# Moving the first block's modulation into the mixing, an embedding's projection ahead of the FFN, and all splits to VectorE

## The chip, the cores and the metric

The kernel runs on one core of a Trainium2 chip. The metric is the device time of one execution in microseconds, the median of several runs. TensorE (PE in the profile) multiplies, with a separate row for its weight loads (PEld); VectorE (DVE), ScalarE (ACT) and GpSimd (POOL) work on elements; SyncE (SP) issues most transfers, GpSimd some.

## What is computed

Two blocks, each with two layers, on 256 tokens of 1024 features. The first block has a mixing layer (a bidirectional scan beside a long convolution) and a neighbourhood attention, each followed by a convolutional FFN and a per-layer embedding. The second block has a context of its own, and everything in it is modulated by a vector computed from a condition:

```python
def conv_ffn(h, norm_g, w_up, conv_w, conv_b, w_down):
    u = dwconv_centred(rmsnorm(h, norm_g) @ w_up, conv_w, conv_b)
    return (jax.nn.gelu(u[..., :D_FF]) * u[..., D_FF:]) @ w_down

def per_layer_embedding(h, p_i, norm_g, w_gate, w_proj):
    return jax.nn.sigmoid(rmsnorm(h, norm_g) @ w_gate) * (p_i @ w_proj)

def half_ffn(h, g, shift, scale, gate, wg, wu, wd):
    return h + 0.5 * gate * swiglu(modulate(rms_norm(h, g), shift, scale), wg, wu, wd)
...
    for l in range(DEPTH):
        ml = jnp.split(s_lat @ w_mod[l] + b_mod[l], N_MOD, axis=-1)
        mc = jnp.split(s_ctx @ w_mod[l] + b_mod[l], N_MOD, axis=-1)
        x = half_ffn(x, g_norm[l, 0], ml[0], ml[1], ml[2], ...)
        ctx = half_ffn(ctx, g_norm[l, 0], mc[0], mc[1], mc[2], ...)
```

The context's first half FFN needs nothing of the first block, so its work can be laid beside that block's. The modulation has 2 x 9 x 1024 results for two conditions; a unit of it is 256 results of a layer, so there are 36 units in a layer.

## The kernel before

Activations lie with features on partitions, as eight tiles of 128 features by 256 tokens. A weight arrives as float32 in a tile `raw`, and is split (`split`, L358) into a rounded high part `wh`, a cast on ScalarE (L359), and a rest `wl` (L360), a subtraction on VectorE or GpSimd. Each step over 128 inputs is three products, high by high, high by low and low by high (`gemm`, L368 to L370; for four tiles at once `gemm_wide`, L406 to L408). Some weights are used unsplit, in plain float32 (`plain_tiles`, L372, and `plain`, L397). An output tile over eight such steps is 24 products, a pair of them 48.

The stages in order are the mixing (0 to 546 us of the trace), the first FFN (to 770), its embedding (to 834), the attention (to 1018), the second FFN (to 1235), its embedding (to 1286), and from there the second block. Behind the mixing's scan, from about 334 us, the context's half FFN runs as filler (`ctx_ffn`, L948, tiles named `fill`). It is a generator that yields after each group of `FILL`: pairs of up tiles, then eight down tiles. In the mixing the loop at L935 takes `CUT` = 4 groups; the rest is drained behind ple1 (L1484 and after), and lies beside the stages between as their scheduler places it. The order of each engine's queue comes from a scheduler at build time; on the chip each queue runs in that order, and instructions wait for their operands and for a free buffer.

In the mixing the split weights of the filler use two buffers each, `wh` and `wl`, in the pool `self.wha` (`whl_open(es, 2, 0)`, L1456); after the mixing the filler has its own pool (`self.own`), and there GpSimd does its subtraction (L360). GpSimd also does half of the subtractions of the first four weight tiles of a stage (`first`, `relief`, L348 to L353), and the sums of squares for the next norm (`sq_add`, L496).

The modulation (`mod_until`, L1004) loads a tile of w_mod, 128x1024, and reduces it against a condition on VectorE (L1032). Two variants are in use. In the mixing `mod_open(pool, aid=False, room=self.wha)` (L847) takes buffers of the same pool as the filler's weights, issues loads on GpSimd's queue (L1029) and makes two reductions for a tile, one for each condition. In the FFNs `aid` is on: the loads are SyncE's, VectorE makes one reduction, and GpSimd multiplies (L1036) and ScalarE sums (L1037) for the second condition. Twelve units are done in the mixing, eight in the first FFN (to 20), six in the second (to 26).

The embedding (`embed`, L572) splits its 256 inputs `p` and the projection's weights, makes the projection `pj` at the start of its stage (16 steps, 48 products), and then the gate's products behind its norm. A norm is a sum over partitions (L454), a chain of small operations for the root (L424 to L441), a transposition (L480), and the scaling (L519).

Of the kernel before, what the change touches and what calls it, by code (L numbers as in the profile page):

```python
# [17 lines left out]
P = 128  # L18
D = 1024
T = 256  # L20
KT = 8
FF = 2816
FT = 22
# [6 lines left out]
M00 = 32  # L30
CUT = 4
DECAY = math.exp(-0.5)

# [239 lines left out]
class Net:  # L273
# [35 lines left out]
    def pieces(self, name, todo):  # L309

        nc, arr = self.nc, self.ap[name]
        i = 0
        while i < len(todo):
# [34 lines left out]
    def first(self, it, n):  # L348

        self.relief = 2  # L350
        tiles = [next(it)[1:] for _ in range(n)]
        self.relief = 0
        return tiles  # L353

    def wtiles(self, name, tiles, kt):
        return self.pieces(name, [(t, 0, kt) for t in tiles])

    def split(self, src, hi, lo, pool=False):  # L358
# [13 lines left out]
    def plain_tiles(self, name, todo):  # L372
# [4 lines left out]
        while i < len(todo):  # L377
# [6 lines left out]
            for c in range(0, n, 512):  # L384
                w = min(512, n - c)
                raw = self.t(self.whole, [P, 512], "raw")
# [100 lines left out]
    def sq_add(self, m, s=0):  # L487
# [43 lines left out]

    def conv_ffn(self, i, mods):
        nc = self.nc
        with ExitStack() as es:
            pool = self.pool(es, "ffn")
            self.whl_open(es, 0, 3)
            it = self.wtiles(f"f_up{i}", range(2 * FT), KT)
            first = self.first(it, 4)
            xh, xl = self.norm1(pool, f"ffn_norm{i}")
            self.mod_open(pool, True)  # L540
            mod0 = self.mod_at
            outs = [self.acc()[:, :T] for _ in range(4)]
            self.gemm_wide(outs, first, KT, xh, xl)
            for k0, kn in GROUPS:
                mh = self.t(pool, [P, 8, T], "mh", F32R)
                ml = self.t(pool, [P, 8, T], "ml", F32R)
                for j in range(kn):
# [14 lines left out]
                    self.split(u[:, 0], mh[:, j], ml[:, j])  # L562
                    if k0 + j > 1:
                        self.mod_until(mod0 + (mods - mod0) * (k0 + j) // (FT - 1))
                for m, wh, wl in self.pieces(f"f_dn{i}", [(m, k0, kn) for m in range(KT)]):
# [3 lines left out]
                    if k0 == 16:  # L569
                        self.sq_add(m)  # L570

    def embed(self, i):  # L572
        nc = self.nc
        with ExitStack() as es:
            pool = self.pool(es, "ple")
            self.whl_open(es, 0, 3)
            ph = self.t(pool, [P, 2, T], "ph", F32R)
            pl = self.t(pool, [P, 2, T], "pl", F32R)
            pr = self.t(pool, [P, 2, T], "pr")
            nc.sync.dma_start(pr, self.ap[f"p{i}"])  # L580
            self.split(pr, ph, pl)
            pj = self.t(pool, [P, KT, T], "pj")
            m = 0
            for _, wh, wl in self.pieces(f"ple_p{i}", [(t, 0, 2) for t in range(KT)]):
                ps = self.acc()
                self.gemm(ps[:, :T], wh, wl, 2, ph, pl)
                nc.scalar.mul(pj[:, m], ps[:, :T], 0.5)
                m += 1
            it = self.wtiles(f"ple_g{i}", range(KT), KT)
# [4 lines left out]
            for m in range(KT):  # L594
# [7 lines left out]
                nc.scalar.activation(s, ps, AF.Tanh, scale=0.5)  # L602
                nc.vector.scalar_tensor_tensor(s, s, 1.0, pj[:, m], op0=ALU.add, op1=ALU.mult)
                nc.vector.tensor_add(self.H[:, m], self.H[:, m], s)
# [234 lines left out]
    def mix(self, ef):  # L839
# [4 lines left out]
        with ExitStack() as es:  # L844
# [4 lines left out]
            with ExitStack() as e2:  # L849
# [587 lines left out]
    def run(self, es, stages=None):  # L1437
# [13 lines left out]
        self.own, self.tables = None, False  # L1451
        self.nsplit = self.relief = 0
        self.spare = []
# [15 lines left out]
        self.nrm = self.pool(es, "nrm", bufs=6)  # L1469
        self.rsp = self.pool(es, "rsp", bufs=2)  # L1470
        ep = es.enter_context(ExitStack())
        self.psum_open(ep, mm=4, aux=2, fill=2)
# [9 lines left out]
        for s in st:  # L1482
            if s.startswith("ffn"):
                self.conv_ffn(int(s[3]), 20 if s == "ffn0" else 26)  # L1484
            elif s.startswith("ple"):
                self.embed(int(s[3]))
                if s == "ple1" and self.own:
                    self.tag = self.aux = "fill"
# [4 lines left out]
                    ep.close()  # L1493
                    self.psum_open(es, mm=5, aux=3)
            elif s == "na":
                self.na()
# [262 lines left out]
```

## Time and profile before

| | us |
|---|---|
| median of three runs | 2905.65 (2905.5 to 2906.85) |
| the profiled execution | 2907.19 |
| its span in the profile | 2905.4 |
| TensorE busy in it | 2767.0 |
| VectorE busy | 1978.3 |
| ScalarE busy | 1216.2 |
| GpSimd busy | 396.7 |
| mean share of the clock that TensorE was granted | 0.97 |

The page gives busy time by engine, slices of the span with the granted clock, the chain that ended last, the costliest groups of instructions and the transfers. The trace behind it answers narrower questions: busy time in given stretches, who ended whose waits, the instructions of a line, and the instructions in order of time. The granted clock is a share of 2.4 GHz; 0.5 is the lower level of 1.2 GHz.

### The profile page before, as it was taken

The numbers are of one execution on the slowest core, as the hardware profiler recorded it, in microseconds if no ns is written. First come the engines' busy times: TensorE is split into PE (matmuls) and PEld (weight loads), VectorE is DVE, ScalarE is ACT, GpSimd is POOL, SyncE is SP. The second block draws the span as 40 slices with busy tenths as digits, with TensorE's granted clock in tenths as the row PEclk, the third lists the DMA queues.
The fourth block names the chain that finished last, engine by engine and source line by source line (L and its number), as shares of the span: only waits on it lengthen the run. The fifth ranks groups of instructions, "written<-read, shape, count | busy, mean of one in ns | idle before, by whom it ended". The sixth has DMA issues, their size and how long they took to land.

```text
span 2905.4 us, 49052 instructions
## 1 busy us (share of the span) xinstructions
PE 2767.0 (95%) x19514; PEld 2441.6 (84%) x19514; DVE 1978.3 (68%) x3569; ACT 1216.2 (42%) x2120; POOL 396.7 (14%) x276
## 2 busy tenths in 40 slices
PE   6998999899999989989999999999999999999999
PEld 4676788899899889979988669888898888895999
DVE  5875755789976688867754665777755655567655
ACT  3212223555545555555554454222243222455543
POOL 0100000322542411221211001000010000121100
PEclk8998999999999999989999999999999999999999
DMA  4441223666455356547732103555535444230564
GB/s 164 126 141 58 81 83 117 211 214 221 165 179 159 107 189 203 185 142 241 223 113 68 47 30 119 186 196 179 163 110 164 141 142 134 79 117 25 175 188 139
DMA packets 150807, 415.91 MB, mean 143 GB/s; under 512 B 31585, under 2 KB 51698, under 8 KB 149682
## 3 DMA queue, kind: packets, MB, share of 16 engines
q1 hardware_dynamic: 146258, 393.89, 42.3%
q0 software_dynamic: 4320, 18.88, 1.9%
q8 instruction: 154, 2.52, 0.4%
q14 instruction: 75, 0.61, 0.1%
HBM read 411.66 MB, written 1.05 MB: 142 GB/s over the span
## 4 chain that ended last, share of the span: by engine, by line
PE 73%; DVE 8%; issue 4%; ACT 2%; DMA 1%; POOL 0%; ACTq 0%; DVEq 0%; SPq 0%; POOLq 0%
PE mm L368 18%; PE mm L370 18%; PE mm L369 18%; DVE wl L360 3%; PE fill L370 2%; PE fill L368 2%; PE mm L407 2%; PE mm L1413 2%; PE fill L369 2%; PE mm L408 2%; PE mm L406 2%; PE mm L1381 1%; PE aux L459 1%; ACT wh L359 1%; PE aux L1407 1%
## 5 line engine op out<-in xcount | busy, mean ns | idle before, releaser
L359 ACT CAST wh<-raw 128x1024 fp32r<-128x1024 f32 (+3 forms) x652 | 606.8, 938 | 1016.3 <-PE mm L369 560.8
L360 DVE TENSOR_TENSOR wl<-raw,wh 128x1024 fp32r<-128x1024 f32 (+3 forms) x582 | 712.6, 1228 | 321.3 <-ACT wh L359 308.4
L368 PE MATMUL mm<-xnh,wh 128*128 128x256 f32 (+1 forms) x2592 | 821.4, 317 | 4.2 <-ACT u L527 3.2
L370 PE MATMUL mm<-xnh,wl 128*128 128x256 f32 (+1 forms) x2592 | 818.5, 316 | 1.9 <-DVE wl L360 1.9
L369 PE MATMUL mm<-xnl,wh 128*128 128x256 f32 (+1 forms) x2592 | 815.5, 315 | 0.4 <-DVE xnl L360 0.2
L368 PEld LDWEIGHTS mm<-xnh,wh 128*128 128x128 f32 x2592 | 488.3, 188 | 38.3 <-ACT u L527 3.4
L370 PEld LDWEIGHTS mm<-xnh,wl 128*128 128x128 f32 x2592 | 488.3, 188 | 37.9 <-DVE wl L360 2.9
L369 PEld LDWEIGHTS mm<-xnl,wh 128*128 128x128 f32 x2592 | 487.9, 188 | 34.4 <-DVE xnl L360 1.0
L369 PE MATMUL mm<-ml,wh 128*128 128x256 f32 (+1 forms) x1104 | 341.3, 311 | 10.8 <-DVE ml L360 10.8
L368 PE MATMUL mm<-mh,wh 128*128 128x256 f32 (+1 forms) x1104 | 340.5, 314 | 5.0 <-ACT mh L359 2.1
L370 PE MATMUL mm<-mh,wl 128*128 128x256 f32 (+1 forms) x1104 | 341.0, 312 | 0.0
L1032 DVE CUSTOM_DVE_ANT_0 junk<-wm,sc,vecs 128x1024 bf16<-128x1024 f32 x200 | 256.8, 1284 | 4.2 <-ACT sc L1015 1.1
L369 PEld LDWEIGHTS mm<-ml,wh 128*128 128x128 f32 x1104 | 208.4, 189 | 25.2 <-DVE ml L360 12.2
L368 PEld LDWEIGHTS mm<-mh,wh 128*128 128x128 f32 x1104 | 206.3, 189 | 18.5 <-ACT mh L359 2.9
L370 PEld LDWEIGHTS mm<-mh,wl 128*128 128x128 f32 x1104 | 208.2, 189 | 13.3
L360 POOL TENSOR_TENSOR wl<-raw,wh 128x1024 fp32r<-128x1024 f32 (+2 forms) x70 | 134.2, 1925 | 370.6 <-DMA raw<-s_up 190.9
L496 POOL TENSOR_TENSOR ss<-ss,xt 128x256 f32<-128x256 f32 x56 | 58.9, 1058 | 889.1 <-issue 689.3
L1036 POOL TENSOR_TENSOR wm<-wm,sc 128x1024 f32<-128x1024 f32 x40 | 109.9, 2747 | 432.3 <-DVE mod L1032 346.6
L1107 DVE SCALAR_TENSOR_TENSOR H<-mm,mod,H 128x256 f32<-128x256 f32 x112 | 53.7, 482 | 116.7 <-PE mm L370 116.6
L1154 DVE TENSOR_TENSOR sg<-sg,mm 128x256 f32<-128x256 f32 (+1 forms) x88 | 48.7, 553 | 123.1 <-PE mm L370 120.8
L407 PE MATMUL mm<-xnl,wh 128*128 128x256 f32 x416 | 121.3, 299 | 7.9 <-DVE xnl L1058 4.9
L408 PE MATMUL mm<-xnh,wl 128*128 128x256 f32 x416 | 120.1, 295 | 3.9 <-DVE wl L360 2.0
(549 smaller groups left out, 4386.9 us busy)
## 6 DMA issues: line engine op xcount, KB each, us to landing
raw<-s_up SPq DMA_DIRECT2D x220, 512.0 KB, 3.7
wm<-w_mod SPq DMA_DIRECT2D x120, 512.0 KB, 4.4
raw<-f_up SPq DMA_DIRECT2D x88, 512.0 KB, 4.5
raw<-s_dn SPq DMA_DIRECT2D x65, 512.0 KB, 3.5
raw<-s_dn SPq DMA_DIRECT2D x60, 384.0 KB, 3.1
raw<-w_in SPq DMA_DIRECT2D x34, 512.0 KB, 3.6
raw<-f_dn SPq DMA_DIRECT2D x32, 512.0 KB, 4.4
raw<-w_in SPq DMA_DIRECT2D x52, 256.0 KB, 3.0
```

Source lines behind the costliest of these rows:

```text
L359: self.nc.scalar.copy(hi, src)
L360: (self.nc.gpsimd if pool or self.own and self.tag == "fill" else self.nc.vector).tensor_sub(lo, src, hi.bitcast(F32))
L368: nc.tensor.matmul(out, wh[:, ws], h, start=first and k == 0, stop=False)
L369: nc.tensor.matmul(out, wh[:, ws], l, start=False, stop=False)
L370: nc.tensor.matmul(out, wl[:, ws], h, start=False, stop=last and k == kt - 1)
L406: nc.tensor.matmul(out, wh[:, s], h, start=k == 0, stop=False)
L407: nc.tensor.matmul(out, wh[:, s], l, start=False, stop=False)
L408: nc.tensor.matmul(out, wl[:, s], h, start=False, stop=k == kt - 1)
L496: (nc.gpsimd if self.tag == "mm" else nc.vector).tensor_add(self.ss[s], self.ss[s], x)
L1032: keep(nc.vector.tensor_tensor_reduce(out=junk, in0=w, in1=self.sc[:, i], scale=0.5 if self.half else 1.0, scalar=self.vecs[:, b + t : b + ...
L1036: nc.gpsimd.tensor_mul(w, w, self.sc[:, 1])
L1413: nc.tensor.matmul(po[64 * h : 64 * h + 64, :T], v(k0 // P + i), pTs[h][:, i], start=i == 0, stop=i == nk // P - 1)
```

## The change

The modulation's units 12 to 25 leave the two FFNs and are done in the mixing, with the mixing's variant, in bursts of three, four, three and four units behind each of the four groups of the filler. The projection of the embedding becomes a function of its own, `project_embedding`, called ahead of the FFN's first weight tiles, with plain float32 products and a result that lives until the embedding. `split` and `sq_add` use VectorE alone. The rest of the filler is drained ahead of the second FFN instead of behind ple1, and the accumulators in PSUM are set up anew there.

```diff
@@ pieces, first, split
-                self.nsplit += 1
-                self.split(raw[:, j * n : (j + 1) * n], hi[:, :n], lo[:, :n], self.relief and self.nsplit % self.relief == 0)
+                self.split(raw[:, j * n : (j + 1) * n], hi[:, :n], lo[:, :n])
...
-        (self.nc.gpsimd if pool or self.own and self.tag == "fill" else self.nc.vector).tensor_sub(lo, src, hi.bitcast(F32))
+        self.nc.vector.tensor_sub(lo, src, hi.bitcast(F32))
@@ sq_add
-            (nc.gpsimd if self.tag == "mm" else nc.vector).tensor_add(self.ss[s], self.ss[s], x)
+            nc.vector.tensor_add(self.ss[s], self.ss[s], x)
@@ conv_ffn
+            self.project_embedding(i)
             it = self.wtiles(f"f_up{i}", range(2 * FT), KT)
             first = self.first(it, 4)
             xh, xl = self.norm1(pool, f"ffn_norm{i}")
-            self.mod_open(pool, True)
-            mod0 = self.mod_at
...
-                    if k0 + j > 1:
-                        self.mod_until(mod0 + (mods - mod0) * (k0 + j) // (FT - 1))
@@ project_embedding (new), embed
+        pr = self.t(self.pjp, [P, 2, T], "pr")
+        nc.sync.dma_start(pr, self.ap[f"p{i}"])
+        self.pj = self.t(self.pjp, [P, KT, T], "pj")
+        for m, w in self.plain_tiles(f"ple_p{i}", [(t, 0, 2) for t in range(KT)]):
+            ps = self.acc()
+            self.plain(ps[:, :T], w, 2, pr)
+            nc.scalar.mul(self.pj[:, m], ps[:, :T], 0.5)
...
-            for _, wh, wl in self.pieces(f"ple_p{i}", [(t, 0, 2) for t in range(KT)]):
-                ps = self.acc()
-                self.gemm(ps[:, :T], wh, wl, 2, ph, pl)
-                nc.scalar.mul(pj[:, m], ps[:, :T], 0.5)
@@ mix
                 self.rest = self.ctx_ffn(fp)
-                for _ in range(CUT):
+                for i in range(CUT):
                     next(self.rest)
+                    self.mod_until(12 + (MODS - 12) * (i + 1) // CUT)
@@ the loop over stages
-                if s == "ple1" and self.own:
+                if s == "ffn1" and self.own:
                     self.tag = self.aux = "fill"
                     for _ in self.rest:
                         pass
```

VectorE's queue behind the second group of the filler, before: the filler's down tiles of one group (`Hc`, the context's sum), and the subtractions for the next group's first weights (`wl`).

```order
L1107 SCALAR_TENSOR_TENSOR Hc_74<-fill_4553,mod_73,Hc_74 128x256
L1107 SCALAR_TENSOR_TENSOR Hc_74<-fill_4568,mod_73,Hc_74 128x256
L360 TENSOR_TENSOR wl_4583<-raw_4580,wh_4582 128x1024
L360 TENSOR_TENSOR wl_4613<-raw_4610,wh_4612 128x1024
L360 TENSOR_TENSOR wl_4652<-raw_4649,wh_4651 128x1024
```

The same place now, where the second burst begins: `in` is the out-projection, `H` its sum, and `junk` the reductions' elementwise result, with w_mod's tiles in `wh` and `wl`.

```order
L1101 SCALAR_TENSOR_TENSOR Hc_74<-fill_4269,mod_73,Hc_74 128x256
L937 TENSOR_TENSOR H_59<-H_59,in_3268 128x256
L493 TENSOR_TENSOR ss_515_3234<-ss_515_3234,xtin_3265 128x256
L937 TENSOR_TENSOR H_59<-H_59,in_3274 128x256
L493 TENSOR_TENSOR ss_515_3234<-ss_515_3234,xtin_3271 128x256
L1026 ISA junk_4282,mod_73<-wh_4280,sc_92,vecs_58 128x1024
L1026 ISA mod_73 128x1
L1026 ISA junk_4284,mod_73<-wh_4280,sc_92,vecs_58 128x1024
```

And its end, where the subtraction for the next group's first weight stands behind the 13th reduction.

```order
L1026 ISA junk_4318,mod_73<-wh_4316,sc_92,vecs_58 128x1024
L1026 ISA mod_73 128x1
L357 TENSOR_TENSOR wl_4332<-raw_4329,wh_4331 128x1024
L1026 ISA junk_4320,mod_73<-wh_4316,sc_92,vecs_58 128x1024
L1026 ISA mod_73 128x1
L1026 ISA junk_4324,mod_73<-wl_4322,sc_92,vecs_58 128x1024
```

Sixteen reductions, each with the reading of its accumulator, have come in between the last sum of one group and the second weight of the next.

TensorE's queue at the same place now, from the last down tile of the group (`fill_4269`) over two plain steps to the next group's first up tile (`fill_4328`), whose third product reads the `wl` above; before, the out-projection's steps lay among the filler's products and the next group followed directly.

```order
L365 MATMUL fill_4269<-mh_4079,wh_4265 128x256
L366 MATMUL fill_4269<-ml_4080,wh_4265 128x256
L367 MATMUL fill_4269<-mh_4079,wl_4266 128x256
L394 MATMUL in_3268<-y_91,raw_3254 128x256
L394 MATMUL in_3274<-y_91,raw_3254 128x256
L365 MATMUL fill_4328<-xnh_3449,wh_4331 128x256
L366 MATMUL fill_4328<-xnl_3450,wh_4331 128x256
L367 MATMUL fill_4328<-xnh_3449,wl_4332 128x256
```

TensorE's queue at the start of the second embedding, before: the norm's sums (`c_sums`), then the projection's products of the split `p` (`ph`), whose 48 stand on both sides of the transposition (`c_ident`).

```order
L454 MATMUL aux_12408<-c_sums_64,xt_12267 128x2 x2
L368 MATMUL mm_12290<-ph_12277,wh_12286 128x256
L368 MATMUL mm_12302<-ph_12277,wh_12298 128x256
L368 MATMUL mm_12314<-ph_12277,wh_12310 128x256
L368 MATMUL mm_12326<-ph_12277,wh_12322 128x256
```

The same place now.

```order
L451 MATMUL aux_13324<-c_sums_64,xt_13290 128x2 x2
L477 MATMUL aux_13347<-c_ident_66,rsyaux_13334 128x128 x2
L403 MATMUL mm_13384<-xnh_13350,wh_13302 128x256
L403 MATMUL mm_13385<-xnh_13350,wh_13308 128x256
L403 MATMUL mm_13386<-xnh_13350,wh_13314 128x256
```

The projection is gone from there: sums, transposition and the gate's products follow one another.

## Rows read from the trace of the kernel before

**Rows 1.** The page's first part: busy us, share of the span, instructions.

```profile
PE 2767.0 (95%) x19514; PEld 2441.6 (84%) x19514; DVE 1978.3 (68%) x3569; ACT 1216.2 (42%) x2120; POOL 396.7 (14%) x276
```

**Rows 2.** Busy time by stretch: stretch, length, engines (instructions), granted clock, DMA share, GB/s.

```profile
426.00:548.00 122.00, 111.85 (x856) 103.43 (x855) 74.46 (x156) 47.74 (x86) 7.74 (x3) 0.94 0.45 146
548.00:770.00 222.00, 210.88 (x1755) 208.81 (x1753) 201.44 (x289) 130.39 (x215) 76.66 (x36) 0.99 0.63 209
770.00:834.00 64.00, 56.35 (x413) 54.53 (x411) 49.16 (x77) 31.70 (x63) 30.00 (x17) 0.89 0.47 155
1018.00:1235.00 217.00, 198.98 (x1622) 194.88 (x1620) 186.32 (x297) 123.79 (x207) 40.74 (x22) 0.98 0.58 193
1235.00:1286.00 51.00, 38.40 (x264) 36.93 (x264) 36.74 (x67) 24.74 (x50) 16.38 (x9) 0.81 0.52 171
```

**Rows 3.** PE's waits, 548 to 1286 us: who ended them, us, times, longest.

```profile
PE aux L454 <- ACT xt L491: 11.1, 6, 3.1
PE mm L369 <- DVE ml L360: 10.8, 7, 3.5
PE aux L454 <- POOL ss L496: 5.1, 2, 3.8
PE aux L480 <- DVE rsyaux L441: 3.8, 3, 2.0
...
PE fill L370 <- POOL wl L360: 2.4, 4, 1.2
...
PE mm L408 <- POOL wl L360: 1.9, 2, 1.4
```

**Rows 4.** Instructions in order of time: start, us, engine, line; DVE, then POOL.

```profile
538.21 2.26 DVE L433 TENSOR_TENSOR rshaux<-rsxaux,rsyaux 128x2 f32<-128x2 f32 x1
540.50 0.16 DVE L434 TENSOR_TENSOR rshaux<-rshaux,rsyaux 128x2 f32<-128x2 f32 x1
...
535.76 4.68 POOL L360 TENSOR_TENSOR wl<-raw,wh 128x1024 fp32r<-128x1024 f32 x2 [190.93 <-DMA raw<-s_up]
```

**Rows 5.** The modulation's lines L1032 and L1029: ns min/median/max, first and last start.

```profile
L1032 DVE DVE_READ_ACCUMULATOR2_ANT mod<- x248: 70/83/85, 103.4 to 2489.4; 128x1 f32 x124
...
L1032 DVE CUSTOM_DVE_ANT_0 junk<-wh,sc,vecs x24: 1262/1278/1286, 102.2 to 183.7; 128x1024 bf16<-128x1024 f32 x24
...
DMA to landing us min/median/max: 3.4/4.4/12.7
```

**Rows 6.** PE in order of time: split products, plain products; then line L397.

```profile
426.00 0.28 PE L368 MATMUL fill<-xnh,wh 128*128 128x256 f32 x1
426.12 0.28 PE L369 MATMUL fill<-xnl,wh 128*128 128x256 f32 x1
...
427.50 2.43 PE L397 MATMUL in<-y,raw 128*128 128x256 f32 x10
...
L397 PE MATMUL in<-y,raw x64: 377/379/483, 328.6 to 493.9; 128*128 128x256 f32 x64
```

**Rows 7.** DVE in order of time: an operation on 128x256, and a whole split.

```profile
534.42 0.48 DVE L1107 SCALAR_TENSOR_TENSOR Hc<-fill,mod,Hc 128x256 f32<-128x256 f32 x1
...
544.97 1.21 DVE L360 TENSOR_TENSOR wl<-raw,wh 128x1024 fp32r<-128x1024 f32 x1
```

**Rows 8.** Busy time by stretch, as in rows 2; and a PE wait from 426 to 548.

```profile
540.00:548.00 8.00, 6.11 (x34) 6.11 (x35) 6.98 (x21) 5.92 (x11) 3.49 (x2) 0.58 0.96 363
...
PE aux L480 <- DVE rsyaux L441: 4.0, 1, 4.0
```

**Rows 9.** POOL's groups, 548 to 1286 us: busy us, mean ns, idle before.

```profile
L360 POOL TENSOR_TENSOR wl<-raw,wh 128x1024 fp32r<-128x1024 f32 x27 | 73.6, 2737 | 82.1 <-ACT wh L359 77.3 <-PE fill L370 3.9 <-PE aux L454 0.9
L1036 POOL TENSOR_TENSOR wm<-wm,sc 128x1024 f32<-128x1024 f32 x28 | 72.0, 2570 | 294.8 <-DVE mod L1032 260.1 <-ACT wh L359 15.7 <-ACT u L560 9.3
```

**Rows 10.** PE in order of time at the second block's start; idle before it in brackets.

```profile
1285.30 0.69 PE L480 MATMUL aux<-c_ident,rsyaux 128*128 128x128 f32 x2 [2.03 <-DVE rsyaux L441]
1287.18 1.22 PE L406 MATMUL mm<-xnh,wh 128*128 128x256 f32 x4 [1.19 <-ACT xnh L1057]
```

More of the change, by code (lines that the diff above doesn't have):

```diff
@@ L31 @@
 CUT = 4
+MODS = 26
 DECAY = math.exp(-0.5)
@@ L348, in first, with split @@
     def first(self, it, n):
[L350 to L353, printed above, removed]
+        return [next(it)[1:] for _ in range(n)]
     def wtiles(self, name, tiles, kt):
         return self.pieces(name, [(t, 0, kt) for t in tiles])
-    def split(self, src, hi, lo, pool=False):
+    def split(self, src, hi, lo):
         self.nc.scalar.copy(hi, src)
-        (self.nc.gpsimd if pool or self.own and self.tag == "fill" else self.nc.vector).tensor_sub(lo, src, hi.bitcast(F32))
+        self.nc.vector.tensor_sub(lo, src, hi.bitcast(F32))
     def gemm(self, out, wh, wl, kt, xh, xl, cols=slice(0, T), x0=0, w0=0, first=True, last=True):
@@ L385, in plain_tiles @@
                 w = min(512, n - c)
-                raw = self.t(self.whole, [P, 512], "raw")
+                raw = self.t(self.whole, [P, 512 if self.tag == "in" else 1024], "raw")
                 src = arr[t : t + m, :, k0 * P + c : k0 * P + c + w].rearrange("t p n -> p t n")
@@ L529, in conv3, with conv_ffn @@
         nc.vector.scalar_tensor_tensor(out[:, 0 : n - 1], src[:, 1:n], w[2], out[:, 0 : n - 1], op0=ALU.mult, op1=ALU.add)
-    def conv_ffn(self, i, mods):
+    def conv_ffn(self, i):
         nc = self.nc
@@ L570, in conv_ffn, with project_embedding @@
                         self.sq_add(m)
+    def project_embedding(self, i):
+        nc = self.nc
+        pr = self.t(self.pjp, [P, 2, T], "pr")
[5 more added lines that the diff above has]
+            nc.scalar.mul(self.pj[:, m], ps[:, :T], 0.5)
     def embed(self, i):
@@ L576, in embed @@
             self.whl_open(es, 0, 3)
[L577 to L583, printed above, removed]
-            for _, wh, wl in self.pieces(f"ple_p{i}", [(t, 0, 2) for t in range(KT)]):
-                ps = self.acc()
-                self.gemm(ps[:, :T], wh, wl, 2, ph, pl)
-                nc.scalar.mul(pj[:, m], ps[:, :T], 0.5)
-                m += 1
             it = self.wtiles(f"ple_g{i}", range(KT), KT)
@@ L602, in embed @@
                 nc.scalar.activation(s, ps, AF.Tanh, scale=0.5)
-                nc.vector.scalar_tensor_tensor(s, s, 1.0, pj[:, m], op0=ALU.add, op1=ALU.mult)
+                nc.vector.scalar_tensor_tensor(s, s, 1.0, self.pj[:, m], op0=ALU.add, op1=ALU.mult)
                 nc.vector.tensor_add(self.H[:, m], self.H[:, m], s)
@@ L1451, in run @@
         self.own, self.tables = None, False
-        self.nsplit = self.relief = 0
         self.spare = []
@@ L1470, in run @@
         self.rsp = self.pool(es, "rsp", bufs=2)
+        self.whole = self.raw
+        fb = es.enter_context(ExitStack())
+        self.pjp = self.pool(fb, "pj")
         ep = es.enter_context(ExitStack())
@@ L1483, in run @@
             if s.startswith("ffn"):
-                self.conv_ffn(int(s[3]), 20 if s == "ffn0" else 26)
-            elif s.startswith("ple"):
-                self.embed(int(s[3]))
-                if s == "ple1" and self.own:
+                if s == "ffn1" and self.own:
                     self.tag = self.aux = "fill"
@@ L1494, in run @@
                     self.psum_open(es, mm=5, aux=3)
+                self.conv_ffn(int(s[3]))
+            elif s.startswith("ple"):
+                self.embed(int(s[3]))
+                if s == "ple1":
+                    fb.close()
             elif s == "na":
```

## The prediction

> **What bounds the kernel now.** I read the page's first part before anything else: TensorE is busy for 2767 of 2905.4 us and VectorE for 1978 [rows 1], so over the whole span the products are the limit and VectorE has room. A mean hides stages, so the second view is busy time by stage [rows 2]. In the last 122 us of the mixing TensorE works 111.9 and VectorE 74.5; in the first FFN VectorE stands at 201 of 222, in the second at 186 of 217; at the two embeddings the granted clock drops to 0.89 and 0.81. The end is therefore set by TensorE's queue, and the time that can be lost or won is TensorE's idle time and its half clock. In the two FFNs and the two embeddings TensorE is idle for 11.1 + 7.7 + 18.0 + 12.6 = 49 us, length less busy time [rows 2]. The third view says who ended these waits [rows 3]: the six kinds shown make 35 of them, and nearly all end with VectorE or ScalarE; where GpSimd is not named it still holds VectorE up: a 128x2 operation that takes 0.16 us took 2.26, and ended as GpSimd's pair of splits did, at 540.5 [rows 4].
>
> **Part 1: 14 units of modulation move into the mixing.** A unit is two tiles of w_mod, and with both conditions on VectorE each tile costs two reductions: 14 x 2 x 2 = 56. One takes 1.28 us and 0.08 for reading its accumulator, 1.36 [rows 5], so VectorE gets 56 x 1.36 = 76 us more in a stretch of 122 in which it has 122 - 74.5 = 47.5 to spare [rows 2]. That doesn't fit, whatever the order. The order makes it worse: the reductions come in four bursts of 12, 16, 12 and 16, one behind each group of the context's FFN, and their tiles use the same two-deep wh and wl buffers as the context's weights, so the next weight tile can't be loaded, cast and split until the burst is nearly through. TensorE has only the out-projection and the scan's small products meanwhile.
>
> The price of burst 2, which has the least beside it: the first tile can be loaded when the second last weight tile before it is released, about 1.1 us (nine products at 0.12 [rows 6]) before TensorE runs dry, and lands 4.4 us after its issue, the median [rows 5]; that leaves 3.3. Then 13 reductions stand ahead of the split of the next weight: 13 x 1.36 = 17.7, and the split 1.21 [rows 7]. TensorE has two plain steps of the out-projection to do, 0.9. Idle: 3.3 + 17.7 + 1.2 - 0.9 = 21 us. Burst 3 has nine ahead of its split and nothing beside it: 3.3 + 12.2 + 1.2 = 17. Burst 1 also has nine ahead, but nine plain steps and six small groups of the scan beside it, some 7 us, and the scan's own VectorE work of 3 to 4 us between: about 14. After each of the three, three more reductions stand ahead of the second weight's split: 3 x 1.36 + 1.2 = 5.3 against 24 products of the first, 2.9; 2.4 each, 7 in all. Sum of idle time 59. Each idle stretch ends at the lower clock: TensorE had waited 4.0 us for rsyaux at 541.9, and the 8 us around it ran at 0.58 of the full 2.4 GHz [rows 8]. 8 x 0.42 = 3.4 us each, **10** for three.
>
> Burst 4 stands beside context products with buffers of their own and beside the first FFN's norm. VectorE's queue from its first reduction to the fourth split of f_up holds 16 reductions (21.8), nine whole splits at 1.21 (10.9) and 41 operations of the size of a 128x256 one (splits of 384 columns, the norm's, the context's), at 0.48 19.7: 52 us [rows 5, 7]; TensorE's over the same has three context tile pairs (3 x 48 x 0.12 = 17.3), 72 smaller products (8.6) and the projection (7.4): 33. That leaves 19, and 3 for the first load: 22, where before there were 4.0 for rsyaux and 1.9 for GpSimd's splits [rows 3, 8]. So **16** more, and 3.4 for the clock. About 3 us of small waits for the context's splits go. Part 1 costs 59 + 10 + 16 + 3 - 3 = **85** us. From below: VectorE's 76 + 74.5 + some 5 for splits that GpSimd had leave 34 over 122, and the wait for the first tile of three bursts adds 10: 44. From above: each first landing at the worst 12.7 us adds 8 x 4 = 32: 117. I take 85, since the order fixes what is queued ahead.
>
> Beside this: a SWDGE load of 512 KB takes about 2.0 us + 524288/436e3 = 3.2 us by the Trainium skill, "DMA: Bandwidth & Descriptors", section on the anatomy of one DMA (an estimate from its fit). The rows have 4.4 as the median over this line's loads, which decides here; by the page the four bursts would be 5 us cheaper.
>
> The FFNs lose for this 28 reductions, 28 GpSimd products of 2.57 us [rows 9] and as many ScalarE sums; none of the three was the last to arrive in many waits of TensorE, so what it gives is in part 3. SyncE's queue loses 28 loads, which were in none of rows 3.
>
> **Part 2: the projection ahead of the FFN.** It becomes 16 plain steps. Ten records of plain products took 2.43 us, and 32 steps of the out-projection (four k of eight tiles) stand as 64 records, so a step is 0.46 us and sixteen are 7.4, against 48 x 0.12 = 5.7 [rows 6]: 1.7 more each, **3.4** in all. The split of p and of eight weights go from VectorE, ScalarE and GpSimd. At the embeddings the 48 products stood between the norm's sums and its transposition, and hid part of the norm. Uncovered is what the next stage shows at its start, 2.0 for rsyaux and 1.2 for xnh [rows 10]: 3.2 each, 6.4; at the second FFN's start the projection covers the same 3.2, and at the first it is counted above. Net **3**.
>
> **Part 3: no splits, no square sums on GpSimd.** GpSimd is busy for 76.7 + 30.0 + 40.7 + 16.4 = 164 us in the four stages [rows 2]; 28 products of 2.57 us, 72, leave for good, and 92 are splits and sums. A whole split takes 2.74 us there and 1.21 on VectorE [rows 7, 9], so VectorE takes some 92 x 0.44 = 40 us over, and loses 28 x 1.36 = 38 and what GpSimd had lengthened. It is loaded no more than before. Which waits go, by rows 3: of the 10.8 for ml 9, of the 5.1 for GpSimd's sums 4, the 4.3 for GpSimd's splits, of the 11.1 for xt (a norm's own length, half of it lengthened) 5, of rsyaux 2, and of the 14 that rows 3 don't show, by the same share of two thirds, 6 to 9: about 31. The clock lost in these stages is 222 x 0.01 + 64 x 0.11 + 217 x 0.02 + 51 x 0.19 = 23 us [rows 2]; the waits of the norms stay, so half comes back: 12. Together **-43**, between -25 (what names GpSimd or ml, and a fifth of the clock) and -72 (all, 49 + 23). What is late next there is the norm's own chain.
>
> Sum on the profiled execution, 2907.2 us: 2907.2 + 85 + 3.4 + 3 - 43 = 2955.6; the median of the runs lies 1.5 under the profiled one, so **2954 us**.
>
> **The rivals.** (a) VectorE's lock gives everything back, and the kernel is faster. The mechanism is the one of the 2.26 us row: without GpSimd's splits every VectorE operation keeps its short time, no edge of a stage has a wait of weight, and the clock stays up: -72. With bursts at their floor, 44 and 7 for two clock drops, and 6 for part 2, the time is 2905.7 + 51 + 6 - 72 = 2891. It decides from the point at which what comes back exceeds what the bursts cost; for it speaks that VectorE ends most of rows 3, against it that all the idle time is 49 us and the norms remain. 9%. By the Trainium skill, "SBUF — State Buffer", section "Who interferes with whom", a VectorE instruction with two SBUF inputs and a GpSimd one that reads SBUF block each other for the whole instruction; rows 4 agree, and the rule by itself says nothing of how much of it lay on TensorE's path.
>
> (b) The two effects meet halfway: bursts at 60, 50 back: 2905.7 + 60 + 6 - 50 = 2922. The scan in burst 1 would hide more, and the loads would land early. 18%.
>
> (c) Loads late: the burst's tiles come on GpSimd's queue while SyncE's queue brings the FFN's weights; at 12.7 us for each first landing, 32 more: 2986. 9%.
>
> (d) It cancels, 2905 +- 6, bursts at 60 and 60 back: 4%. The forecast keeps 60%.
>
> **How the numbers follow.** The forecast alone spans about 2930 to 2975. Taking in (b) and most of (c) gives 2912 to 2985; beyond lie (a), (d) and the end of (c). Faster by over 0.2% (5.8 us, about what a measurement can tell) has (a) and a little of (d): 0.10. Within 0.2%: 0.04. Slower: the rest, 0.86.
>
> **What would show it.** In the trace of after: three gaps of TensorE of 14 to 21 us between 426 and 600, ended by a weight's wl or wh, with runs of L1026 reductions on VectorE over the same time, and a half clock after each; a first FFN that starts some 85 us later; stages from there to the second transposition of ple1 shorter by 25 to 72 in sum; 128x2 operations of the norm's root at 0.16 us. The forecast is wrong if the mixing grows by less than 50 us, which says that the bursts are hidden, or if the FFNs shrink by more than their waits, which says that something besides TensorE's idle time and clock was lost there.

## The result and the profile after

The changed kernel takes 2934.84 us (median; 2932.51 to 2936.92) against 2905.98 of the kernel before: the ratio is 1.0099, 95% interval 1.0081 to 1.0116. It is 28.9 us slower. The forecast was 2954, slower by 48, with 2912 to 2985 as its range.

The page's first part, the answer to [rows 1]:

```profile
PE 2762.9 (94%) x19482; PEld 2434.8 (83%) x19482; DVE 1983.7 (68%) x3710; ACT 1179.4 (40%) x2042; POOL 137.3 (5%) x139
```

TensorE is as busy as before, 2763 against 2767 us, in a span that is 28.7 longer (2934.1): the time is idle time of TensorE. To place it, both traces are cut at the same instructions, the transposition in each norm. First the kernel before, then the changed one; the columns are those of [rows 2].

```profile
426.00:541.90 115.90, 105.75 (x823) 97.33 (x821) 69.08 (x143) 42.51 (x76) 4.68 (x2) 0.96 0.42 134
541.90:783.40 241.50, 228.33 (x1851) 225.50 (x1852) 215.95 (x322) 143.31 (x241) 86.45 (x39) 0.97 0.63 208
783.40:834.40 51.00, 45.01 (x348) 43.99 (x346) 40.28 (x57) 24.00 (x48) 23.66 (x15) 0.93 0.50 163
834.40:1024.70 190.30, 184.71 (x1415) 166.60 (x1415) 139.48 (x302) 100.52 (x209) 70.03 (x48) 0.99 0.50 153
1024.70:1240.70 216.00, 201.03 (x1635) 197.58 (x1636) 183.47 (x297) 123.89 (x207) 36.12 (x17) 0.98 0.56 186
1240.70:1285.30 44.60, 32.73 (x236) 31.95 (x234) 33.20 (x52) 22.15 (x43) 16.38 (x9) 0.83 0.55 181
1285.30:2905.40 1620.10, 1590.58 (x9458) 1377.52 (x9458) 1015.25 (x1761) 649.13 (x1088) 142.54 (x117) 0.98 0.42 135
```

```profile
426.00:603.10 177.10, 124.83 (x891) 115.05 (x892) 127.48 (x241) 45.03 (x77) 12.81 (x25) 0.82 0.51 168
603.10:848.60 245.50, 237.50 (x1962) 234.09 (x1961) 194.00 (x326) 134.09 (x216) 1.06 (x2) 1.00 0.62 200
848.60:886.30 37.70, 36.07 (x299) 35.20 (x298) 29.66 (x72) 17.57 (x38) 0.00 (x0) 1.00 0.43 131
886.30:1078.70 192.40, 177.82 (x1340) 158.47 (x1339) 144.12 (x326) 98.53 (x207) 20.21 (x8) 0.98 0.47 139
1078.70:1278.20 199.50, 192.45 (x1603) 191.28 (x1603) 149.25 (x254) 109.97 (x173) 0.00 (x0) 0.97 0.56 177
1278.20:1314.70 36.50, 28.96 (x210) 27.84 (x210) 23.77 (x54) 16.13 (x32) 0.57 (x1) 0.83 0.41 133
1314.70:2934.10 1619.40, 1586.60 (x9458) 1373.33 (x9458) 1036.27 (x1806) 649.10 (x1088) 85.38 (x72) 0.98 0.42 135
```

Lengths alone mislead, since the filler and the projection lie in other stages now. Idle time, length less TensorE's busy time, doesn't: 10.2 to 52.3 us at the mixing's end (+42.1), 13.2 to 8.0 in the first FFN, 6.0 to 1.6 in its embedding, 5.6 to 14.6 in the attention (+9.0), 15.0 to 7.1 in the second FFN, 11.9 to 7.5 in its embedding, 29.5 to 32.8 behind. The seven add up to +32.6, and busy time fell by 3.9: 28.7, the difference of the spans. So the mixing lost 42 and the FFNs and embeddings gave 22 back; the attention lost 9 and the second block (the last row of either fence) 3, which no term of the prediction had. The first FFN's 8.0 all lie in its first 42 us, where the fourth burst ends.

The mixing's loss is the bursts. TensorE in order of time at the second one and the third, idle time in brackets:

```profile
507.77 0.58 PE L365 MATMUL fill<-xnh,wh 128*128 128x256 f32 x1 [17.46 <-ACT wh L356]
508.15 0.42 PE L366 MATMUL fill<-xnl,wh 128*128 128x256 f32 x1
511.77 0.58 PE L367 MATMUL fill<-xnh,wl 128*128 128x256 f32 x1 [3.21 <-DVE wl L357]
512.15 0.42 PE L365 MATMUL fill<-xnh,wh 128*128 128x256 f32 x1
512.37 0.41 PE L366 MATMUL fill<-xnl,wh 128*128 128x256 f32 x1
...
557.42 0.58 PE L365 MATMUL fill<-xnh,wh 128*128 128x256 f32 x1 [14.54 <-ACT wh L356]
...
561.35 0.58 PE L367 MATMUL fill<-xnh,wl 128*128 128x256 f32 x1 [3.13 <-DVE wl L357]
```

And VectorE over the same time: the first tile lands, and the split of the filler's next weight stands behind the 13th reduction.

```profile
493.33 1.28 DVE L1026 CUSTOM_DVE_ANT_0 junk<-wh,sc,vecs 128x1024 bf16<-128x1024 f32 x1 [2.00 <-DMA wh<-w_mod]
...
509.28 1.29 DVE L1026 CUSTOM_DVE_ANT_0 junk<-wh,sc,vecs 128x1024 bf16<-128x1024 f32 x1
510.49 0.08 DVE L1026 DVE_READ_ACCUMULATOR2_ANT mod<- 128x1 f32 x1
510.49 1.22 DVE L357 TENSOR_TENSOR wl<-raw,wh 128x1024 fp32r<-128x1024 f32 x1
```

The reductions come at 1.33 us each. At each burst TensorE's wait is told in two rows, because its order has two products ahead that need only `wh`. After it the products follow at 0.22 us, not the 0.12 of [rows 6]: the clock's lower level.

### The profile page after: what moved, and what is told of

It reads as the page before. It is cut to its first block, busy times and chain, and to the rows that moved or that the text cites. A ratio compares the mean times of both kernels' runs of the same rounds, so it can differ in the third digit from the quotient of the medians.

```text
span 2934.1 us, 48781 instructions
## 1 busy us (share of the span) xinstructions
PE 2762.9 (94%) x19482; PEld 2434.8 (83%) x19482; DVE 1983.7 (68%) x3710; ACT 1179.4 (40%) x2042; POOL 137.3 (5%) x139
## 4 chain that ended last, share of the span: by engine, by line
PE 71%; DVE 6%; issue 3%; DMA 2%; ACT 1%; SPq 0%; ACTq 0%; DVEq 0%; POOLq 0%
PE mm L367 19%; PE mm L366 19%; PE mm L365 19%; PE mm L404 2%; PE mm L405 2%; PE mm L1407 2%; PE mm L403 2%; DVE wl L357 2%; PE mm L1375 1%; PE aux L456 1%; PE fill L367 1%; PE fill L365 1%; PE fill L366 1%; PE aux L1401 1%; ACT wh L356 1%
## 5 line engine op out<-in xcount | busy, mean ns | idle before, releaser
L365 PEld LDWEIGHTS mm<-xnh,wh 128*128 128x128 f32 x2592 | 488.2, 188 | 38.6 <-issue 2.3
L1026 DVE CUSTOM_DVE_ANT_0 junk<-wm,sc,vecs 128x1024 bf16<-128x1024 f32 x172 | 220.3, 1281 | 3.7 <-ACT sc L1009 1.3
L365 PE MATMUL fill<-xnh,wh 128*128 128x256 f32 x352 | 107.1, 304 | 33.2 <-ACT wh L356 33.2
L403 PE MATMUL mm<-xnh,wh 128*128 128x256 f32 x416 | 112.2, 301 | 7.6 <-ACT xnh L1051 4.0
L367 PE MATMUL fill<-xnh,wl 128*128 128x256 f32 x352 | 107.3, 305 | 11.1 <-DVE wl L357 11.0
```

Of the source, the lines that this page charges most:

```text
L365: nc.tensor.matmul(out, wh[:, ws], h, start=first and k == 0, stop=False)
L367: nc.tensor.matmul(out, wl[:, ws], h, start=False, stop=last and k == kt - 1)
L403: nc.tensor.matmul(out, wh[:, s], h, start=k == 0, stop=False)
L1026: keep(nc.vector.tensor_tensor_reduce(out=junk, in0=w, in1=self.sc[:, i], scale=0.5 if self.half else 1.0, scalar=self.vecs[:, b + t : b + ...
```

## The experiments

Theory A is the prediction's: the bursts cost some 60 us at the mixing's end, and what comes back later comes from GpSimd's leaving (part 3). Theory B is its rival for the second half: what comes back comes from the modulation's leaving the FFNs. Each part was undone or done alone.

**Part 1 undone (e1).** The changed kernel, modulation back in the FFNs:

```diff
-                    self.mod_until(12 + (MODS - 12) * (i + 1) // CUT)
...
+            self.mod_open(pool, True)
+            mod0 = self.mod_at
...
+                    if k0 + j > 1:
+                        self.mod_until(mod0 + (mods - mod0) * (k0 + j) // (FT - 1))
```

> The changed kernel with part 1 alone undone: units 12 to 25 are back in the two FFNs (GpSimd products, ScalarE sums). Theory A (the bursts cost what TensorE lost from 426 to 645 us, 83 against 22, so 62; what came back later came from parts 2 and 3): 2935 - 62, and some 8 for GpSimd's products that hold VectorE again: about 2880. Theory B (what came back later came from the modulation leaving the FFNs): 2935 - 62 + 30 = about 2903.

Measured: 2902.13 us (2895.25 to 2915.55), 0.9989 of before, interval 0.9973 to 1.0005. Theory B's number. Part 1 costs 33 us on top of the others, not 55, and parts 2 and 3 together give 4 us, which the interval can't tell from nothing.

**Part 3 alone (e2).** The kernel before, with

```diff
-        (self.nc.gpsimd if pool or self.own and self.tag == "fill" else self.nc.vector).tensor_sub(lo, src, hi.bitcast(F32))
+        self.nc.vector.tensor_sub(lo, src, hi.bitcast(F32))
...
-            (nc.gpsimd if self.tag == "mm" else nc.vector).tensor_add(self.ss[s], self.ss[s], x)
+            nc.vector.tensor_add(self.ss[s], self.ss[s], x)
```

> The kernel before with part 3 alone: every split and square sum on VectorE, modulation and projection where they were. Theory A: of the 34 us that came back behind the mixing, part 3 gave most: about 2882, faster than before by 20 to 30. Theory B (the modulation's leaving gave it): 2900 to 2906. A third theory (VectorE, at 201 of 222 us in the first FFN, becomes the bound when splits are added to its reductions): 2910 or more.

Measured: 2909.44 us (2899.05 to 2918.05), 1.0012, interval 0.9999 to 1.0024: no gain. Theory A's second half falls. The first FFN, the attention, the second FFN and what lies behind the second embedding:

```profile
545.20:792.30 247.10, 236.03 (x1948) 234.22 (x1947) 219.01 (x356) 149.43 (x251) 40.06 (x16) 0.98 0.63 211
...
839.00:1020.60 181.60, 170.70 (x1309) 152.53 (x1307) 141.10 (x326) 95.49 (x199) 18.99 (x9) 1.00 0.48 143
1020.60:1241.70 221.10, 206.54 (x1626) 203.05 (x1627) 181.91 (x296) 124.01 (x206) 30.65 (x12) 0.93 0.56 183
...
1281.80:2908.00 1626.20, 1591.50 (x9458) 1377.44 (x9458) 1036.39 (x1806) 649.28 (x1088) 86.30 (x72) 0.98 0.42 134
```

With the embeddings' 4.4 and 8.3 us, idle time in the two FFNs and embeddings is 38 us, 8 less than before; but the attention idles 10.9 us where it had 5.6, and the rest 34.7 where it had 29.5. The third theory isn't borne out: VectorE is busy for 219 of 247 us in the first FFN, 216 of 241.5 before, and TensorE idles less there.

**Part 1 alone (e3).** The kernel before, without modulation in the FFNs and with the loop of the changed kernel behind the filler's groups:

> The kernel before with part 1 alone: 14 units in bursts in the mixing, splits and sums half on GpSimd as before. Theory A: 2906 + 62, less some 10 for GpSimd's 28 products that no longer hold VectorE: about 2958. Theory B: 2906 + 62 - 30 = about 2938.

Measured: 2950.0 us (2945.43 to 2951.3), 1.0147, interval 1.0132 to 1.0162. Between the theories. Two rows of its trace say what part 1 gives by itself: the FFNs, to be held against those of before above.

```profile
598.00:847.00 249.00, 234.99 (x1932) 232.89 (x1933) 199.82 (x307) 129.96 (x212) 50.24 (x30) 0.97 0.58 187
...
1084.00:1287.00 203.00, 197.25 (x1632) 196.02 (x1632) 149.12 (x259) 109.04 (x181) 3.75 (x4) 0.97 0.53 166
```

In the second FFN the idle time falls from 15.0 to 5.8 us with GpSimd's relief still there, and the stage from 216 to 203 with the same number of products: that gain is the modulation's. In the first it isn't seen: the fourth burst runs into its start, and 14 us are idle.

**Part 2 alone (e4).** The kernel before, with `project_embedding` ahead of the FFN's first weights, its pool, and the filler drained ahead of the second FFN, all as in the changed kernel:

> The kernel before with part 2 alone: plain projection ahead of each FFN, the filler drained ahead of the second FFN. By the prediction's term 3.4 + 3: about 2912. Theory C (the projection's leaving shortened the embeddings, where TensorE lost 10 and 17 us before and 3 and 12 after): 2894.

Measured: 2919.94 us (2910.45 to 2925.65), 1.0039, interval 1.0027 to 1.0051: 13 us by the medians, 8 to 15 by the interval, where the term was 6. The parts alone sum to 44 + 3 + 13 = 60 and together cost 29, so they interact.

**The bursts without the filler's buffers (e5).** Theory S says that part 1's price is the shared ring, not VectorE's 76 us. The 28 tiles get three buffers of their own:

```diff
+                self.modw = self.pool(es, "modb", side="right")
                 for i in range(CUT):
                     next(self.rest)
...
-                    w = self.t(self.modw, [P, D], ("wh", "wl")[j])
+                    w = self.t(self.modw, [P, D], ("wh", "wl")[j], bufs=None if self.modw is self.wha else 2 - j)
```

> The changed kernel, but the 28 tiles of the bursts get three buffers of their own in place of the filler's wh and wl; the scheduler then lays the 56 reductions among the scan's small operations, ahead of the filler. Theory S (the price of part 1 is the bursts: the shared buffers hold the filler's next weight back until the reductions are through): VectorE has 334 - 225 = 109 us to spare in the first 334, so the mixing grows by 10 to 25 instead of 62, and the time is 2885 to 2900. Theory W (VectorE's 76 us are the price wherever they stand, since the scan's chains go through VectorE): 2925 or more.

Measured: 2890.36 us (2887.73 to 2892.95), 0.9935, interval 0.9917 to 0.9954. 44 us less than the changed kernel and faster than before. Busy time of this kernel, then of the changed one, while the scan runs:

```profile
200.00:334.00 134.00, 108.64 (x758) 83.41 (x756) 118.08 (x258) 27.76 (x54) 12.17 (x23) 0.81 0.49 157
```

```profile
200.00:334.00 134.00, 123.42 (x926) 94.21 (x921) 71.79 (x183) 34.09 (x68) 0.00 (x0) 0.85 0.20 62
```

VectorE does 51 of the 56 reductions here (the other five lie just ahead), 118 us of work where it had 72, and had the room. TensorE falls back by some 170 records, plain and split, and does them later. The edit takes the buffers apart and so lets the scheduler place the reductions elsewhere; which of the two did how much wasn't tried. What falls is the theory that VectorE's work costs its time wherever it stands.

**Half of a burst's work (e6).** The changed kernel, the second condition over 128 columns:

```diff
+                    c = P if self.modw and self.mod_at > 12 and i else D
                     keep(nc.vector.tensor_tensor_reduce(
-                        out=junk, in0=w, in1=self.sc[:, i], ...
+                        out=junk[:, :c], in0=w[:, :c], in1=self.sc[:, i, :c], ...
```

> The changed kernel, but the second condition's reduction of the 14 moved units is over 128 of 1024 columns only (that part of the modulation is left out): 28 reductions of about 0.3 us instead of 1.28, so VectorE has 27 us less in the bursts and the loads are the same. Theory S1 (a burst's idle time is the number of reductions ahead of the next split times 1.36): of 9 + 13 + 9 and about 8 ahead half are short, 19 us less: about 2915. Theory S2 (the loads of the tiles through two buffers set a burst's length, one landing of 4.4 us for two tiles): 5 us less at most, 2930.

Measured: 2926.52 us (2919.58 to 2933.65), 1.0061, interval 1.0040 to 1.0081. Between the two numbers, and its runs spread over 14 us, so the total doesn't decide. The trace, of the fastest of them, does:

```profile
426.00:584.70 158.70, 120.13 (x867) 108.14 (x866) 104.55 (x236) 44.20 (x76) 12.17 (x23) 0.87 0.54 174
```

TensorE idles 38.6 us from 426 to the first FFN's transposition where the changed kernel idles 52.3, and 6.2 against 8.0 in the first FFN: 15 us less, three times what theory S2 allows and near S1's 19. The reductions ahead of the split set more of a burst's length than the loads do.

**Both conditions on VectorE in the FFNs (e7).** On top of the first experiment:

```diff
-            self.mod_open(pool, True)
+            self.mod_open(pool, True, aid=False)
```

> As e1 (modulation in the FFNs, the rest as changed), but both conditions' reductions on VectorE: no GpSimd products, no ScalarE sums. Theory L (what TensorE loses in the FFNs with modulation, 24 us in the second, comes from GpSimd's products that hold VectorE): 2902 - 10 to 15 = about 2889. Theory V (it comes from VectorE's load, to which 38 us are added): 2910 or more.

Measured: 2906.7 us (2898.18 to 2911.71), 0.9992, interval 0.9981 to 1.0003: as the first experiment, within their spreads. Neither theory's number comes. The FFNs and the attention, first of e1, then of this one:

```profile
550.00:798.00 248.00, 238.10 (x1960) 236.29 (x1959) 224.40 (x352) 151.55 (x248) 39.64 (x16) 0.97 0.66 218
...
836.00:1029.00 193.00, 178.10 (x1343) 158.84 (x1341) 141.46 (x326) 98.25 (x207) 21.09 (x9) 0.98 0.48 144
1029.00:1242.00 213.00, 196.10 (x1603) 192.53 (x1603) 184.09 (x292) 125.05 (x199) 28.91 (x12) 0.97 0.59 194
```

```profile
550.00:803.00 253.00, 248.46 (x2059) 247.12 (x2058) 224.84 (x389) 140.03 (x226) 0.00 (x0) 0.97 0.69 226
...
849.00:1037.00 188.00, 163.96 (x1182) 143.45 (x1181) 131.10 (x304) 89.49 (x192) 17.47 (x8) 0.94 0.42 125
1037.00:1243.00 206.00, 194.99 (x1602) 191.79 (x1602) 177.08 (x305) 111.93 (x175) 0.00 (x0) 0.96 0.62 202
```

Without GpSimd's products TensorE idles 11 us less in the two FFNs (9.9 + 16.9 to 4.5 + 11.0). But a hundred records of the filler went into the first FFN, 1960 to 2059, and were missing in the attention, whose idle time rose from 14.9 to 24.0 at a lower clock.

**The first weights' relief (e8).** In the changed kernel the attention's idle time ends with the row

```profile
1078.71 0.69 PE L477 MATMUL aux<-c_ident,rsyaux 128*128 128x128 f32 x2 [7.30 <-DVE rsyaux L438]
```

at the second FFN's start, and VectorE shows three splits between the steps of the root's chain (two of them here):

```profile
1074.17 1.23 DVE L357 TENSOR_TENSOR wl<-raw,wh 128x1024 fp32r<-128x1024 f32 x1
1075.32 0.15 DVE L433 TENSOR_TENSOR rsaaux<-rsaaux,rshaux 128x2 f32<-128x2 f32 x1
1075.51 0.16 DVE L434 SCALAR_TENSOR_TENSOR rsyaux<-rsaaux,rsyaux 128x2 f32<-128x2 f32 x1
1075.68 1.22 DVE L357 TENSOR_TENSOR wl<-raw,wh 128x1024 fp32r<-128x1024 f32 x1
```

So every second of these splits was given back to GpSimd, by the lines of `first`, `pieces` and `split` that the change had removed, without the filler's.

> The changed kernel, but every second subtraction of a stage's first four weights is GpSimd's again. Theory Q (the wait of 7.3 us for rsyaux at the second FFN's start is three splits queued between the steps of the root's chain): that wait falls to 3 to 5, others of the kind by 1 to 2, against 1 to 2 for GpSimd's lock: 2935 - 3 = 2932. Rival: nothing there changes or the lock costs more: 2935 to 2942.

Measured: 2938.87 us (2932.58 to 2940.69), 1.0104, interval 1.0083 to 1.0126. No gain. The wait fell to 5.2 us, but a wait of 5.2 for `xnh` came behind it. The cause lay further up.

**Own buffers without part 2 (e9), and alone (e10).** The first is e5's edit on part 1 and part 3, the second on part 1 alone.

> As e5 (own buffers, reductions beside the scan, all splits on VectorE), but the projection in its embedding and the filler drained behind it, as before. Theory P (part 2 costs time: alone 13 us, most of it at the second FFN's start): 2890 - 10 = about 2880. Theory P2 (with all splits on VectorE part 2 gives, as e1 against e2, 7 us): about 2897.

Measured: 2883.16 us (2881.07 to 2887.68), 0.9928, interval 0.9911 to 0.9944. By the medians part 2 costs 7 us here; the intervals of e5 and e9 overlap, but the traces say where it lies: the attention, up to the second FFN's transposition, idles 16.8 us in e5 and 9.1 in e9.

> The kernel before with part 1 alone, with own buffers. Theory S: the bursts' price leaves e3's time as it left the changed kernel's (2935 to 2890): 2950 - 45 = about 2905. Theory S': GpSimd's splits do less harm when the modulation has left the FFNs, and part 2 costs 13: about 2885.

Measured: 2888.53 us (2886.27 to 2894.09), 0.9944, interval 0.9929 to 0.9959. So shared buffers cost 61 us where part 1 stands alone (2950 to 2888.5), and part 3 gives some 5 us where the modulation has left the FFNs (2888.5 to 2883.2), about as much as the runs of one kernel differ by. Its FFNs settle who gave the time back, with GpSimd's splits and sums still there:

```profile
559.00:776.00 217.00, 214.87 (x1809) 214.47 (x1808) 166.62 (x266) 123.11 (x204) 31.27 (x17) 0.99 0.60 185
776.00:823.00 47.00, 38.08 (x292) 36.82 (x291) 38.34 (x56) 20.84 (x42) 23.74 (x15) 0.92 0.55 169
...
1014.00:1223.00 209.00, 205.53 (x1741) 204.73 (x1740) 158.52 (x273) 117.06 (x203) 19.35 (x21) 1.00 0.54 166
```

Idle time in the FFNs is 2.1 and 3.5 us, where the kernel before has 13.2 and 15.0. (The second also holds a hundred more records of the filler than before, 1741 against 1635; e3's, with 1632, has 5.8.) In the embedding it is still 8.9; with all splits on VectorE, in e9, it is 2.6:

```profile
778.00:826.00 48.00, 45.45 (x369) 44.87 (x369) 36.72 (x74) 24.68 (x48) 0.69 (x1) 0.96 0.65 195
```

In the second embedding it is 13.3 in e10 and 8.5 in e9. The modulation costs the FFNs, GpSimd's splits and sums the embeddings.

**The projection's loads (e11, e12).** SyncE's queue in e5 ahead of the second FFN shows why the splits of f_up come late: the projection's four loads take the four raw buffers, and f_up's begin some 20 us later.

```profile
993.91 7.09 SPq L385 DMA_DIRECT2D raw<-ple_p  x4
1015.29 14.09 SPq L323 DMA_DIRECT2D raw<-f_up  x8
```

Two kernels put the projection behind the first weights, and behind the norm:

```diff
-            self.project_embedding(i)
             it = self.wtiles(f"f_up{i}", range(2 * FT), KT)
             first = self.first(it, 4)
+            self.project_embedding(i)
```

> As e5, with the projection called behind the FFN's first four weights instead of ahead of them, so its p and its weights (which take the four raw buffers) no longer hold back the loads of f_up. Theory R (at the second FFN's start the splits of f_up stand between the steps of the root's chain because their loads came late): the wait of 8.4 us for rsyaux there falls to 2 to 4, and the time to 2890 - 6 = 2884. Rival (the chain is just uncovered there, since the filler is gone): the wait stays over 6, 2890 as e5.

Measured: 2884.5 us (2880.88 to 2886.59), 0.9923, interval 0.9906 to 0.9940. The wait in e5, and what it became:

```profile
1030.56 0.69 PE L477 MATMUL aux<-c_ident,rsyaux 128*128 128x128 f32 x2 [8.44 <-DVE rsyaux L438]
```

```profile
1024.55 0.43 PE L477 MATMUL aux<-c_ident,rsyaux 128*128 128x128 f32 x2 [1.47 <-DVE rsyaux L438]
```

The median is 6 us lower, as expected. The intervals of e5 and e11 overlap, so it is the wait that shows it, and not the total.

> As e5, with the projection called behind the norm, which lays all 16 plain steps between the norm's sums and its transposition. Theory R: as e11, and 7 us of products cover the chain, the wait under 1: 2882. Rival: the projection's loads, now behind the first weights, come late themselves and TensorE waits for them in place of rsyaux: 2888 or more.

Measured: 2883.71 us (2873.58 to 2898.34), 0.9938, interval 0.9919 to 0.9957. The wait for rsyaux is gone, and one of 1.7 for `xnh` remains. Its runs spread too far to tell it from e11 or e9. All three, at 2883 to 2885, are faster than both kernels.

## Why the prediction was right, and where its steps were off

**What bounds the kernel** held: busy time stayed, and the whole difference is TensorE's idle time, in the places named but for 12 us (9 in the attention, 3 behind the second embedding). The first FFN starts 61 us later (603.1 against 541.9), not 85.

**Bursts 2 and 3** held, burst 1 was set too high. Forecast idle 14, 21 and 17 and 2.4 for each second weight; measured 8.8 (26 us from 426, 17.2 busy), 20.7 and 17.7. From the last product before it to the first with the new `wl`, burst 1 took 17 us, 8 of them work, where the sum had some 20 with 7. The answer for the last two:

```profile
490.00:516.00 26.00, 5.33 (x24) 4.73 (x23) 23.41 (x38) 2.93 (x4) 2.91 (x6) 0.54 0.55 189
...
542.00:568.00 26.00, 8.34 (x43) 7.84 (x42) 19.36 (x31) 3.14 (x3) 3.18 (x6) 0.61 0.50 166
```

The terms were those that the trace shows: the first tile's landing, reductions ahead of the split, the split. A reduction takes 1.33 with its accumulator, not 1.36, since the reading starts before the reduction's own record ends (510.49, against 509.28 + 1.29). The 2.4 for the second weight wasn't there: at the lower clock the first weight's products last longer and cover it.

**Burst 4** is the term that was most mis-sized. The forecast had 22 us of idle time; the 55 us from 590 to 645, the burst and the first FFN's start, have 9.9. With this row stand those of the whole end of the mixing, and, in a fence of its own, the like stretch of the kernel before:

```profile
590.00:645.00 55.00, 45.08 (x300) 41.37 (x300) 49.01 (x97) 20.53 (x39) 4.24 (x8) 0.94 0.68 227
...
426.00:645.00 219.00, 158.73 (x1122) 145.54 (x1123) 164.87 (x312) 62.41 (x113) 13.87 (x27) 0.85 0.54 174
```

```profile
426.00:557.00 131.00, 118.92 (x912) 110.10 (x911) 83.46 (x162) 50.35 (x89) 16.11 (x5) 0.95 0.46 149
```

The sum set VectorE's 52 us against 33 of TensorE. VectorE was busy for 49, near the forecast; but TensorE was busy for 45: 5 of them ahead of the burst's first reduction at 596.7, and 40 with the work of the sum, whose split products came some 0.15 us apart and not 0.12, partly at the lower clock. From the two rows that start at 426, part 1 costs 60.3 - 12.1 = 48 us of idle time at this end, where the working had 81 - 9 = 72.

**The clock's terms** were about met, 13 us at the bursts and 12 back behind them. An estimate from the traces, TensorE's busy time times the share of the clock that it wasn't granted meanwhile, gives 14.8 us from 426 to 603.1 against 3.4 from 426 to 541.9 before, 11 more; and from there to the second block 6.9 against 20.5, 14 back. So TensorE's busy time as a whole didn't rise. Of the low shares of the clock in the rows (0.54, 0.61) the larger part lies in the gaps themselves.

**Part 3** is the step that failed. It gave 43 us to GpSimd's leaving, read off waits that end with VectorE. (GpSimd itself ends 9.4 of the 35 us in [rows 3], a quarter, where the prediction says that nearly all end with VectorE or ScalarE.) e2, which takes GpSimd's splits and sums away and leaves the modulation in the FFNs, gives nothing: 8 of the 31 us come back in the FFNs and embeddings, and 10 are lost in the attention and behind them. The size was nearly met: counted from the burst's end (645, and 557 before), FFNs and embeddings idle 28 us less, where the working had 31 besides the clock. But the source was wrong: e3's second FFN and both of e10's lose most of their idle time while GpSimd still splits, so in the FFNs it is mostly the modulation's leaving; the splits' share is in the embeddings. The prediction had seen that and given it no term of its own, since none of its instructions was named as a releaser in many waits. Theory L, that GpSimd's products are what holds the FFNs up, has e7's 11 us there for it and no gain in the total. Which part of the modulation it is, VectorE's reductions, GpSimd's products, ScalarE's sums or the loads, stays open. An operation on two tiles took 2.26 us in place of 0.16 beside GpSimd's splits [rows 4]. By the Trainium skill, "SBUF — State Buffer", section "Who interferes with whom", a VectorE instruction with two SBUF inputs contends with a GpSimd instruction that reads SBUF; that row agrees. What taking all of GpSimd's splits and sums away is worth once the modulation has left is e9 against e10: some 5 us. It has a price, too, that no term had: behind the second embedding TensorE idles 31.9 to 34.7 us in the kernels with all splits and sums on VectorE, 29.2 to 30.8 in those that kept GpSimd's (before, e3, e4, e10).

**Part 2** had the term 6 and measured 13 alone and some 7 in e9 against e5. The 3.4 for plain products may stand. Of the two norms that it was to uncover by 3.2 each, the second embedding's shows (at 1278.2 in the changed kernel: 4.3 us for rsyaux, 1.0 for xnh), the first's hardly, since the filler's products lie beside it. What failed is the step "at the second FFN's start the projection covers the same 3.2". It uncovered 7 to 8 us there: its loads took the raw buffers and f_up's splits moved into the root's chain. e11 shows it by undoing the order alone. In the changed kernel this wait is 7.3 us, and 1.1 before: 6 of the 9 us that the attention lost.

**The rivals.** (a), the lock gives everything back, is out by the result: with GpSimd nearly idle in the FFNs and embeddings, 24 of their 46 us of idle time remain, and by e2 its splits and sums alone give nothing. (b), bursts at 60 and 50 back, came nearest in its sum (2922 against 2935) but had the same wrong source. (d), that it cancels, is out by the 28.9 us; with part 2's 6, which it left out, its own sum would have been 2912. (c), late loads, is out by the wait of VectorE for the bursts' tiles from 426 to 640, three times, 11.0 us in all, where 10 were counted:

```profile
DVE junk L1026 <- DMA wh<-w_mod: 11.0, 3, 4.7
```

The forecast's 48 against 29 is so one large error, the bursts with 24 us of idle time too many (12 of them in burst 4, 8 in burst 1); busy time that is 8 lower than in the sum (4 less than before, where it had 4 more); and smaller errors the other way: 6 more for part 2's place ahead of the second FFN and the attention, 3 in part 3, 3 behind. That the time still lay in the range is in part luck: the errors partly cancel, and the 28 us that came back did so mainly for a reason that the prediction had not priced.

## What to carry to other kernels

Work that is moved into a stage with room still needs its own buffers: where it shares a ring with the stream that feeds TensorE, the stream stops for the length of the burst, and the room isn't used. (With buffers of its own the work here also went to another place in the order, and how much either of the two gave was not separated.) The engine named as the releaser is only the end of a queue; ask what stands ahead of the releasing instruction in that queue before giving its wait to a neighbour. And a step moved ahead of a stage takes its loads along: here four loads in a ring of four held the next stage's weights back by some 20 us in e5 (15 in the changed kernel), and the price appeared in a norm's chain.

## What the runs showed that was not expected

A filler is a fixed stock. In e7 the first FFN lost half of its idle time, used a hundred more records of the filler, and the attention idled 9 us more: time won in one stage of this chain was lost in the next. That the missing filler is the cause is read from this one pair of traces and was not tested by itself. And the parts don't add: 44, 3 and 13 us alone, 29 together. Parts 2 and 3 together give 4 with the modulation in the FFNs (2906.5 to 2902.1, not clear of the noise) and 15 with it in the bursts (2950.0 to 2934.8).
